# Second FFN's seven-product phase: the block sums move from GpSimd to VectorE

## The chip, the cores and the metric

The kernel runs on one core of a Trainium2 chip. A core has TensorE for matrix products, VectorE and ScalarE for elementwise work, GpSimd for the same at a slower rate, and SyncE, whose queue starts the transfers from memory. Each engine works through its own queue of instructions in order, and engines wait for each other with semaphores. The metric is the device time of one execution in microseconds (us), the median of several runs.

## The reference

One transformer layer over 512 latent and 256 context tokens of width 1024, in float32: a half-step SwiGLU FFN, a token mixer (latent attention with eight heads beside a chunked gating MLP), and a second half-step FFN. Each is modulated by vectors that a third projection makes from a condition. Only the latent stream is returned. The part that matters here is the last:

```python
def swiglu(h, w1, w3, w2):
    return (jax.nn.silu(h @ w1) * (h @ w3)) @ w2

def ffn_sublayer(h_in, shift, scale, gate, norm_w, w1, w3, w2):
    h = modulate(rms_norm(h_in, norm_w), shift, scale)
    return h_in + 0.5 * gate * swiglu(h, w1, w3, w2)
```

In the second FFN, h has 512 rows, and w1 and w3 are 1024 x 2816, so there are 22 column tiles of 128 (NF = 22).

## The kernel before

**Split operands.** TensorE multiplies in a reduced form of float32. To keep the accuracy, every operand is split in two: ScalarE casts it to that form (the high part, tiles `oph`, `hh`, `gh`), and VectorE subtracts the high part from the original (the low part, `opl`, `hl`, `gl`). One product is three matmuls, high x high, high x low and low x high (`mm3`). `Stream.operand` does the two steps of a split for a piece of 128x512 weights; five pairs of operand tiles go round (`OPS = 5`). So splits can run at most five operands ahead of the products that use them.

**Seven products in place of eight.** For column tile f, w1 and w3 together form a 2 x 2 arrangement of blocks of 512 x 128 against the token halves and the depth halves. The class `Winograd` computes the four results with seven products. It needs sums of the weight blocks. With q[0] to q[3] the four 128x512 pieces of one loaded block, the sums are s1 = q2 + q3, then q2 = q0 - q2 (called s3), q0 = s1 - q0 (s2), and q1 = q1 - q0 (s4); each overwrites its piece, once the piece itself was split. On the other side the sums of activations (T1 to T4) are made once. The order of a unit's products in `unit` is T1, B21, T2, T3, then B11 of the next unit, then T4 and B22. T1 multiplies s1, B21 q1, T2 the new q0, T3 the new q2, T4 q3, and B22 the new q1.

**Slots.** `Flow` keeps a queue of wants, functions that each issue one split. Before the matmuls of each product, `Flow.slot` issues, in this order: the first part of the work that evacuates the product before, the splits for which operand tiles have come free, and the rest of the evacuation. The phase is recorded with `nc.ordered = "all"`, so that every engine's queue has the order of this program. Evacuation works on banks of 128x256: VectorE adds banks to each other (`u2`, `u3`, `ev_lo`, `ev_hi`), ScalarE applies silu and the cast of the result `gh`, VectorE makes `gl`. T4 accumulates into the bank of T3; it may start once `ev_u3` has read that bank.

**Who makes the sums.** In `wants`, `first` loads the block (`prep`) and gives GpSimd s1, and behind the split of q0 it gives GpSimd s3 and s2. `third` gives GpSimd s4 behind the split of q1. The first block of the second FFN (f = 4) is an exception: `wino.prep(NPLAIN2, nc.vector)` runs earlier, and its sums s1, s3, s2 and s4 go to VectorE. Column tiles 0 to 3 use plain products. Units 4 to 21 use the seven-product form. After units 4, 8, 12, 16 and 18, `down_flow` runs a down projection whose weights pass through the same wants; each takes 8 slots. In the last unit (`f + 1 == NF`) the order of products is T2, T3, B21, T1, T4, B22, and some matmuls of the final down projection stand among them, where the scheduler put them.

**Transfers.** A block is 1 MB, loaded by SyncE's queue (L127). Two block buffers exist (`BLOCKS = 2`), so the load for unit f + 2 waits until the last piece of unit f's block was split.

The first FFN has a phase of the same class, with 384 columns and GpSimd's sums. It is not part of the change.

The lines that the prediction's steps touch:

```python
    def split(self, dst, src, eng=None):
        self.pin(self.nc.scalar.copy(dst[0], src))
        self.pin((eng or self.nc.vector).tensor_sub(dst[1], src, dst[0].bitcast(F32)))
...
            def ev_u3():
                v.tensor_add(u3, W, u2)
                v.tensor_add(u3, Z, u3)
                yield
```

Of the kernel before, what the change touches and what calls it, by code (L numbers as in the profile page):

```python
# [21 lines left out]
NF = FF // P  # L22
# [151 lines left out]
def layer_kernel(ctx: ExitStack, tc: tile.TileContext, xT, wfirst, wst, wada, wuq, wkpe, cols, wrope, vnw, rope, out):  # L174
    nc = Core(tc)
# [6 lines left out]
    st = Stream(nc, raws, opp, OPS, wst)  # L182
# [81 lines left out]
    u0, rw0 = st.raw_pool.tile([P, 2048], F32, tag="block", bufs=BLOCKS, name="block_first"), st.raw()  # L264
# [48 lines left out]
    def ada_row(r, d, kts=range(NK)):  # L313
        n = 2 * P if d in ROWS2 else P
        o = pa[0:2, :n]
        for kt in kts:
            pin(nc.tensor.matmul(o, sc[:, kt, :], r[:, kt * n : kt * n + n], start=kt == 0, stop=kt == NK - 1))
        return o
# [83 lines left out]
    class SsqAcc:  # L402
        def __init__(self, pool, n, eng):
            self.pool, self.n, self.eng = pool, n, eng
            self.acc = None
            self.squares = []
# [122 lines left out]
    for k in range(NK):  # L529
# [13 lines left out]
        if later:  # L543
            o = ada_row(units[k + 2][0], k + 2)
# [121 lines left out]
    U_UP2 = U_IN + 22  # L666
# [11 lines left out]
    class Winograd:  # L678


        def __init__(self, pool, n, u0, blocks, g_tile, sl_bufs, s1_bufs):
            self.sl_bufs, self.s1_bufs = sl_bufs, s1_bufs
            self.ready = (None,)
            self.pool, self.n, self.u0, self.blocks, self.g_tile = pool, n, u0, blocks, g_tile

# [12 lines left out]
        def wants(self, f):  # L698
            q, s1, eng = [], [], []

            def first():
                if self.ready[0] != f:
                    self.prep(f)
                q[:], s1[:], eng[:] = self.ready[1], [self.ready[2]], [self.ready[3]]
                a = st.operand(q[0])
                if not self.ready[4]:
                    eng[0].tensor_sub(q[2], q[0], q[2])
                eng[0].tensor_sub(q[0], s1[0], q[0])
                return a

            def third():
                a = st.operand(q[1])
                eng[0].tensor_sub(q[1], q[1], q[0])
                return a

            of = lambda i: lambda: st.operand(q[i])
            return first, lambda: st.operand(s1[0]), third, of(0), of(2), of(3), of(1)

        def plan(self, flow, f0, downs, late=False):
# [139 lines left out]
    blocks = {"B11": hb(0, 0), "B21": hb(4, 0), "B22": hb(4, 384), "T1": hb(0, 384)}  # L859
# [51 lines left out]
    wino = Winograd(gp, 384, U_UP1, blocks, g_tile, 1, 4)  # L911
# [29 lines left out]
    for f in range(NFIRST, NPLAIN1):  # L941
        last = f == NPLAIN1 - 1
# [4 lines left out]
        for w in range(2):  # L947
            pair = None
            for g in (1, 0) if last else (0, 1):
# [12 lines left out]
                for k in range(NK):  # L962
                    c = slice(k % 4 * P, k % 4 * P + P)
                    a = [t[:, c] for t in pair[k // 4]]
# [660 lines left out]
    f2 = f2ctx.enter_context(tc.tile_pool(name="ffn2", bufs=2))  # L1625
# [74 lines left out]
    evac(0, 1)  # L1700
    diffs(3)
    blocks = {"B11": B11, "B21": B21, "B22": B22, "T1": T1, "T2": T2, "T3": T3, "T4": T4}
    wino = Winograd(f2, 256, U_UP2, blocks, g2_tile, 2, 2)
    wino.prep(NPLAIN2, nc.vector)
    flow = Flow(OPS)
    wino.plan(flow, NPLAIN2, lambda f: [(CHUNKS2[ci], U_DN2 + starts2[ci]) for ci in ends2(f)])
# [141 lines left out]
```

## Time and profile before

| | |
|---|---|
| median of 3 runs | 1158.27 us (1157.82 to 1159.63) |
| profiled execution | 1157.46 us |
| its span, first to last instruction | 1155.7 us |
| granted TensorE clock | 1.00 |
| TensorE busy | 1137.7 us (98%) |
| VectorE busy | 904.5 us (78%) |
| ScalarE busy | 532.7 us (46%) |
| GpSimd busy | 321.6 us (28%) |

The span is what the profile covers; the time of the execution has 1.76 us more around it. A group of instructions is written as engine, operation, output tile <- input tiles, shape, count, then busy time and the mean of one in ns. In the timeline the first column is the start in us from the span's beginning, the second the duration, and the bracket holds the idle time of the engine ahead of the instruction and what ended it. PE is TensorE, DVE VectorE, ACT ScalarE, POOL GpSimd. Most lines carry L60, the line of a helper that records every instruction, so groups are told apart by their tiles. In the windows each engine has its busy time in the stretch with the number of its instructions.

### The profile page before, as it was taken

The numbers are of one execution on the slowest core, as the hardware profiler recorded it, in microseconds if no ns is written. First come the engines' busy times: TensorE is split into PE (matmuls) and PEld (weight loads), VectorE is DVE, ScalarE is ACT, GpSimd is POOL, SyncE is SP. The second block draws the span as 40 slices with busy tenths as digits, with TensorE's granted clock in tenths as the row PEclk, the third lists the DMA queues.
The fourth block names the chain that finished last, engine by engine and source line by source line (L and its number), as shares of the span: only waits on it lengthen the run. The fifth ranks groups of instructions, "written<-read, shape, count | busy, mean of one in ns | idle before, by whom it ended". The sixth has DMA issues, their size and how long they took to land. (4 is left out here: it accounts for less than half of the span.)

```text
span 1155.7 us, 18702 instructions
## 1 busy us (share of the span) xinstructions
PE 1137.7 (98%) x7070; PEld 1069.7 (93%) x7070; DVE 904.5 (78%) x1670; ACT 532.7 (46%) x1075; POOL 321.6 (28%) x277
## 2 busy tenths in 40 slices
PE   9999999999999999999999999999999999999998
PEld 5699999999999999999988788999999989898997
DVE  4778989888988878867746969869876959686884
ACT  4454431441344213444735549876553535353441
POOL 0001402320433013300017636670013425152330
PEclk9999999999999999999999999999999999999999
DMA  9440244344234665312242101002221322233312
GB/s 346 150 157 24 92 146 147 109 145 154 103 128 146 222 205 170 133 64 68 83 146 91 57 35 56 20 1 76 72 92 55 134 86 77 106 110 110 110 37 92
DMA packets 34650, 125.89 MB, mean 109 GB/s; under 512 B 3584, under 2 KB 10496, under 8 KB 29056
## 3 DMA queue, kind: packets, MB, share of 16 engines
q1 hardware_dynamic: 34416, 124.63, 31.4%
q8 instruction: 56, 0.92, 0.3%
q14 instruction: 34, 0.28, 0.1%
q10 hardware_dynamic: 144, 0.06, 0.0%
HBM read 122.58 MB, written 2.10 MB: 108 GB/s over the span
## 5 line engine op out<-in xcount | busy, mean ns | idle before, releaser
L60 POOL TENSOR_TENSOR block<-block 128x512 f32<-128x512 f32 x69 | 104.9, 1520 | 395.8 <-DVE opl L60 393.1
L60 DVE TENSOR_TENSOR opl<-block,oph 128x512 fp32r<-128x512 f32 x216 | 184.0, 858 | 32.1 <-ACT oph L60 30.0
L60 ACT CAST oph<-block 128x512 fp32r<-128x512 f32 x216 | 133.8, 621 | 144.4 <-PE mm L60 99.1
L60 PE MATMUL mm<-gh,oph 128*128 128x384 f32 (+1 forms) x440 | 155.2, 353 | 0.0
L60 PE MATMUL mm<-gl,oph 128*128 128x384 f32 (+1 forms) x440 | 154.9, 352 | 0.0
L60 PE MATMUL mm<-gh,opl 128*128 128x384 f32 (+1 forms) x440 | 154.9, 352 | 0.0
L60 DVE SCALAR_TENSOR_TENSOR x<-mm,g,x 128x256 f32<-128x256 f32 (+2 forms) x184 | 82.8, 489 | 48.5 <-PE mm L60 47.8
L60 ACT CAST oph<-raw 128x512 fp32r<-128x512 f32 x106 | 64.5, 619 | 93.4 <-PE mm L60 74.5
L60 POOL TENSOR_TENSOR block<-s,block 128x512 f32<-128x512 f32 x35 | 48.2, 1378 | 153.8 <-DVE opl L60 153.1
L60 PEld LDWEIGHTS mm<-gh,oph 128*128 128x128 f32 x440 | 82.6, 188 | 5.7
L60 PEld LDWEIGHTS mm<-gh,opl 128*128 128x128 f32 x440 | 82.6, 188 | 5.6
L60 PEld LDWEIGHTS mm<-gl,oph 128*128 128x128 f32 x440 | 82.6, 188 | 5.5
L60 DVE TENSOR_TENSOR opl<-raw,oph 128x512 fp32r<-128x512 f32 x106 | 71.0, 683 | 11.7 <-ACT oph L60 11.2
L60 PE MATMUL mm<-hl,oph 128*128 128x384 f32 x192 | 64.3, 335 | 0.9 <-DVE hl L60 0.9
L60 PE MATMUL mm<-hh,oph 128*128 128x384 f32 x192 | 64.5, 336 | 0.0
L60 PE MATMUL mm<-hh,opl 128*128 128x384 f32 x192 | 64.1, 334 | 0.0
L60 DVE SCALAR_TENSOR_TENSOR junk<-raw,cb 128x1024 bf16<-128x1024 f32 x48 | 63.2, 1331 | 0.0
L60 POOL TENSOR_TENSOR s<-block 128x512 f32<-128x512 f32 x34 | 51.1, 1504 | 19.8 <-DMA block<-wst 19.8
L60 PE MATMUL one<-hh,oph 128*128 128x384 f32 x144 | 48.1, 334 | 0.0
L60 PE MATMUL one<-hl,oph 128*128 128x384 f32 x144 | 48.1, 334 | 0.0
L60 PE MATMUL one<-hh,opl 128*128 128x384 f32 x144 | 48.1, 334 | 0.0
L60 DVE SCALAR_TENSOR_TENSOR raw<-raw,cb 128x1024 f32<-128x1024 f32 x32 | 41.0, 1287 | 7.6 <-DMA raw<-wada 7.4
(649 smaller groups left out, 3462.7 us busy)
## 6 DMA issues: line engine op xcount, KB each, us to landing
raw<-wst SPq DMA_DIRECT2D x77, 512.0 KB, 3.7
block<-wst SPq DMA_DIRECT2D x36, 1024.0 KB, 4.9
raw<-wada SPq DMA_DIRECT2D x56, 512.0 KB, 4.1
block<-wada SPq DMA_DIRECT2D x7, 1024.0 KB, 7.2
x<-xT SPq DMA_DIRECT2D x6, 512.0 KB, 7.0
raw<-wfirst SPq DMA_DIRECT2D x8, 256.0 KB, 6.2
out<-x SPq DMA_DIRECT2D x7, 256.0 KB, 2.5
block_first<-wada SPq DMA_DIRECT2D x2, 512.0 KB, 8.1
```

The source lines that it names most:

```text
L60: return lambda *a, **k: self.tc.keep_in_program_order(f(*a, **k))
```

## The change

The second FFN's object of class `Winograd` gets `on_vector = True`. All four block sums of its units are then VectorE's, in other places of the program. s1 follows the split of the block's first piece; s3 follows the split of s1, s2 that of q1, and s4 that of the new q0. Each thus stands one want ahead of the split that reads it. In the last unit s1, s3 and s2 follow the first split together, since the order of products differs there. Everything that ScalarE and SyncE issue keeps its order. 68 sums leave GpSimd's queue (four for each of 17 units) and join VectorE's; unit 4's sums stay on VectorE and move by a slot.

```diff
     class Winograd:
-        def __init__(self, pool, n, u0, blocks, g_tile, sl_bufs, s1_bufs):
-            self.sl_bufs, self.s1_bufs = sl_bufs, s1_bufs
+        def __init__(self, pool, n, u0, blocks, g_tile, sl_bufs, s1_bufs, on_vector=False):
+            self.sl_bufs, self.s1_bufs, self.on_vector = sl_bufs, s1_bufs, on_vector
             self.ready = (None,)
             self.pool, self.n, self.u0, self.blocks, self.g_tile = pool, n, u0, blocks, g_tile
...
                 return a
             of = lambda i: lambda: st.operand(q[i])
+            v = nc.vector
+            def sum_s1():
+                s1.append(self.tmp("s1", 512, self.s1_bufs))
+                v.tensor_add(s1[0], q[2], q[3])
+            def sub(d, a, b):
+                v.tensor_sub(q[d], s1[0] if a is None else q[a], q[b])
+            s3, s2, s4 = (2, 0, 2), (0, None, 0), (1, 1, 0)
+            last = f + 1 == NF
+            def first_v():
+                if self.ready[0] == f:
+                    q[:], s1[:] = self.ready[1], [self.ready[2]]
+                else:
+                    r = st.block(wst, (self.u0 + 2 * f) // 2)
+                    q[:] = [r[:, i * 512 : i * 512 + 512] for i in range(4)]
+                o = st.operand(q[0])
+                if not s1:
+                    sum_s1()
+                if last:
+                    sub(*s3)
+                    sub(*s2)
+                return o
+            def then(src, *d):
+                def want():
+                    o = st.operand(src())
+                    if d:
+                        sub(*d)
+                    return o
+                return want
+            if self.on_vector:
+                S1, Q = lambda: s1[0], [lambda i=i: q[i] for i in range(4)]
+                if last:
+                    return first_v, then(S1), then(Q[1], *s4), then(Q[0]), then(Q[2]), then(Q[3]), then(Q[1])
+                return first_v, then(S1, *s3), then(Q[1], *s2), then(Q[0], *s4), then(Q[2]), then(Q[3]), then(Q[1])
             return first, lambda: st.operand(s1[0]), third, of(0), of(2), of(3), of(1)
         def plan(self, flow, f0, downs, late=False):
...
     evac(0, 1)
     diffs(3)
     blocks = {"B11": B11, "B21": B21, "B22": B22, "T1": T1, "T2": T2, "T3": T3, "T4": T4}
-    wino = Winograd(f2, 256, U_UP2, blocks, g2_tile, 2, 2)
+    wino = Winograd(f2, 256, U_UP2, blocks, g2_tile, 2, 2, True)
     wino.prep(NPLAIN2, nc.vector)
     flow = Flow(OPS)
     wino.plan(flow, NPLAIN2, lambda f: [(CHUNKS2[ci], U_DN2 + starts2[ci]) for ci in ends2(f)])
```

## The prediction

> **What bounds the kernel now.** I read the page's busy shares first, then busy time by stage over the second FFN, then VectorE's timeline of one unit, then the instruction groups of the same stretch.
>
> ```profile
> PE 1137.7 (98%) x7070; PEld 1069.7 (93%) x7070; DVE 904.5 (78%) x1670; ACT 532.7 (46%) x1075; POOL 321.6 (28%) x277
> ```
>
> TensorE is busy for 98% of the span; the changed stretch has to be seen alone. A unit is one column tile f of the second FFN in the seven-product phase: seven products T1, B21, T2, T3, B11 (of the next unit), T4, B22. Units come in stretches of 4, 4, 4, 2 and 3 (f 5 to 21), with down projections between them; f 4 stands alone before.
>
> ```profile
> core 0: us, PE busy (x) PEld busy (x) DVE busy (x) ACT busy (x) POOL busy (x), PEclk, DMA share, GB/s
> 880.95:922.26 41.31, 40.93 (x338) 40.46 (x336) 35.93 (x61) 22.08 (x46) 18.68 (x13) 1.00 0.30 105
> 944.04:985.39 41.35, 40.98 (x337) 40.45 (x336) 35.99 (x61) 22.10 (x46) 18.60 (x13) 1.00 0.30 105
> 922.26:944.04 21.78, 21.78 (x98) 18.02 (x97) 12.23 (x20) 5.80 (x12) 4.16 (x3) 1.00 0.27 93
> 1070.32:1090.64 20.32, 20.32 (x169) 20.20 (x168) 17.04 (x29) 10.77 (x22) 6.83 (x5) 1.00 0.31 110
> 1101.55:1121.82 20.27, 20.27 (x169) 20.20 (x168) 16.88 (x29) 10.79 (x22) 7.85 (x6) 1.00 0.15 53
> ```
>
> Windows: the first two rows are stretches of four units, the third the down projection between them, the last two the two-unit stretch and the first two units of the three-unit one. The granted clock is 1.00 throughout. TensorE's own pace and its late places stand in its timeline:
>
> ```profile
> 896.78 0.28 PE L60 MATMUL one<-b11h,oph 128*128 128x256 f32 x1
> 898.32 0.36 PE L60 MATMUL mm<-t4h,oph 128*128 128x256 f32 x1
> ...
> 906.90 0.28 PE L60 MATMUL one<-t3h,opl 128*128 128x256 f32 x1
> 907.02 0.28 PE L60 MATMUL mm<-b11h,oph 128*128 128x256 f32 x1
> 908.34 0.28 PE L60 MATMUL mm<-b11h,opl 128*128 128x256 f32 x1
> 908.82 0.36 PE L60 MATMUL one<-t4h,oph 128*128 128x256 f32 x1 [0.20 <-DVE u L60]
> ...
> 917.53 0.28 PE L60 MATMUL one<-b11h,oph 128*128 128x256 f32 x1
> 919.31 0.35 PE L60 MATMUL mm<-t4h,oph 128*128 128x256 f32 x1 [0.18 <-DVE u L60]
> ```
>
> Matmuls start 0.12 us apart, so a product of 12 takes 1.44 us and a unit of seven 10.08. T4 is late: due at 908.34 + 0.12 = 908.46, it starts at 908.82, because its bank is still read by the addition `u`, which VectorE does late. From the first matmul of B11 to that of T4 the three late units of this stretch take 1.54, 1.80 and 1.78, which is 0.10, 0.36 and 0.34 too long. A stretch of four units should take 28 x 1.44 = 40.32 us and takes 41.31 to 41.35: 1.0 lost, the 0.80 just read and some 0.06 at each restart. Two units should take 20.16: 0.16 lost in 20.32, 0.11 in 20.27. In all 3 x 1.02 + 0.16 + 0.11 = 3.3 us. No gain from this change can be larger.
>
> One whole unit on VectorE, from the addition u = bank + p to the next such addition:
>
> ```profile
> start us, us, engine line op out<-in xcount [idle before <-releaser]
> 907.33 0.41 DVE L60 TENSOR_TENSOR u<-one,p 128x256 f32<-128x256 f32 x1
> 907.67 0.67 DVE L60 TENSOR_TENSOR opl<-s,oph 128x512 fp32r<-128x512 f32 x1
> 908.27 0.87 DVE L60 TENSOR_TENSOR u<-one,u 128x256 f32<-128x256 f32 x2
> 909.05 1.28 DVE L60 TENSOR_TENSOR opl<-block,oph 128x512 fp32r<-128x512 f32 x2
> 910.53 0.43 DVE L60 TENSOR_TENSOR one<-one,u 128x256 f32<-128x256 f32 x1 [0.20 <-PE one L60]
> 911.00 0.43 DVE L60 TENSOR_TENSOR one<-one,sl 128x256 f32<-128x256 f32 x1
> 911.34 0.70 DVE L60 TENSOR_TENSOR opl<-block,oph 128x512 fp32r<-128x512 f32 x1
> 911.96 0.41 DVE L60 TENSOR_TENSOR gl<-one,gh 128x256 fp32r<-128x256 f32 x1
> 912.30 0.41 DVE L60 TENSOR_TENSOR one<-one,u 128x256 f32<-128x256 f32 x1
> 913.05 1.16 DVE L60 TENSOR_TENSOR opl<-block,oph 128x512 fp32r<-128x512 f32 x1 [0.34 <-ACT oph L60]
> 914.13 0.42 DVE L60 TENSOR_TENSOR one<-one,u 128x256 f32<-128x256 f32 x1
> 914.99 0.43 DVE L60 TENSOR_TENSOR gl<-one,gh 128x256 fp32r<-128x256 f32 x1 [0.44 <-ACT gh L60]
> 915.51 2.38 DVE L60 TENSOR_TENSOR opl<-block,oph 128x512 fp32r<-128x512 f32 x2
> 917.82 0.41 DVE L60 TENSOR_TENSOR u<-mm,p 128x256 f32<-128x256 f32 x1
> ```
>
> This unit took 917.82 - 907.33 = 10.49 us, 0.41 above TensorE's 10.08. In the middle of a stretch VectorE's queue sets the pace; in the down projection it is busy 12.23 of 21.78 us and catches up, which is why the first unit of a stretch loses nothing.
>
> **The change, part by part.** GpSimd's four block sums of a unit go to VectorE. Their two prices:
>
> ```profile
> L60 DVE TENSOR_TENSOR opl<-block,oph 128x512 fp32r<-128x512 f32 x106 | 95.5, 909 | 14.6 <-ACT oph L60 12.7
> L60 DVE TENSOR_TENSOR opl<-raw,oph 128x512 fp32r<-128x512 f32 x36 | 24.3, 682 | 1.1 <-ACT oph L60 0.9
> L60 POOL TENSOR_TENSOR block<-block 128x512 f32<-128x512 f32 x33 | 50.4, 1527 | 145.5 <-DVE opl L60 144.2
> L60 ACT CAST oph<-block 128x512 fp32r<-128x512 f32 x106 | 65.7, 622 | 62.8 <-PE mm L60 43.2 <-PE one L60 16.1 <-DMA block<-wst 3.4
> ...
> 840.69 0.69 DVE L60 TENSOR_TENSOR opl<-block,oph 128x512 fp32r<-128x512 f32 x1
> 841.30 0.68 DVE L60 TENSOR_TENSOR block<-block 128x512 f32<-128x512 f32 x1
> 842.01 1.67 DVE L60 TENSOR_TENSOR block<-s,block 128x512 f32<-128x512 f32 x1
> ```
>
> Groups between 849 and 1150 us, then VectorE's timeline at 840 us, where the first block's sums already run on VectorE. *Removed:* GpSimd's instructions, and with them the slowing of VectorE's splits: 909 ns a split from the block, 682 where GpSimd is idle. *Added:* four 128x512 sums on VectorE, 0.68 us alone (841.30). Consecutive independent instructions overlap: two splits last 1.28, so the second starts 0.60 after the first, and that is what a sum takes of the queue; directly behind the sum that it reads it takes 0.71 (841.30 to 842.01). A 256-wide addition takes 0.34 (907.33 to 907.67).
>
> Steady unit, from 10.49 us: the splits at 913.05 and 915.51 ran beside GpSimd. They take 914.13 - 913.05 = 1.08 and 917.82 - 915.51 = 2.31, against 0.60 and 1.21 alone: -1.58. The idle 0.20 (VectorE waiting for TensorE) and 0.34 (for a split whose block came late) fill up once VectorE is the late one: -0.54. Four sums: 4 x 0.605 = +2.42. That is 10.79.
>
> To it comes a wait that is new. The sum q0 = s1 - q0 is written just ahead of the split of q0, and VectorE's queue holds nothing between the two. "One slot ahead" is a slot of the program; with VectorE behind, it is no time. ScalarE's cast must follow the sum, and the split's subtraction the cast. The row at 914.99 shows such a round trip: idle 0.44 for a 256-wide cast (0.37). For 512, with the 0.62 of the cast row, 0.69 idle, and the overlap of 0.08 is lost too: +0.77. Behind the waiting split stand the sum for q1 and the two additions that T4's bank and gate output need. The other sums have an addition or another split between them and their reader; I take their waits at nothing and the cover is VectorE's own work of 0.34 to 0.9 us; uncovered, each costs up to the same 0.77. Steady period: 11.56, so 1.48 us behind TensorE per unit.
>
> Who pays: T4 of the second, third and fourth unit of a stretch. The first of them pays less by what is left of the lead (up to five operands), 0.27 (before, the first lost 0.16 and the second 0.43, with 0.06 to 0.07 for the restart): 1.21. The middle: 1.48. The last has a plain down operand where a sum would stand ahead of `u`, so 0.60 less: 0.88. Sum 3.57, less 1.02 lost already: +2.55, three times +7.65. The two-unit stretch has one such T4, first and last at once: 1.21 - 0.60 = 0.61, less 0.16: +0.45. The last three units have one, in the second; there the last block's three sums are issued together, two dependent ones at 0.71 more: 0.61 + 1.42 = 2.03, less 0.11: +1.9. Unit 4, the last unit (matmuls of the final down projection stand among its own) and the down projections pay nothing: their cover is VectorE's 9 idle us per projection; gone, a unit would cost 1.48.
>
> Queues: SP's order is unchanged. Each block load still waits for VectorE's last split of the block two before. The chain that ended last shows how long it takes from there:
>
> ```profile
> 896.94 4.89 DMA block<-wst
> ```
>
> A unit that stretches to 11.56 us gives the load more time, so I cost it at nothing; if it came as late as the 0.34 seen at 913.05, it would cost 0.34 a unit. ScalarE's order is unchanged; GpSimd has nothing else to do here, so its relief itself brings nothing.
>
> Sum: 7.65 + 0.45 + 1.9 = **+10.0 us**. The profiled execution took 1157.46 us (span 1155.70 and 1.76 around it), the median of the runs 1158.27, 0.81 above: 1167.5 on the first, 1168.3 on the second.
>
> Bounds: without the new round trip each late T4 is 0.77 cheaper: stretches of four 0.44 + 0.71 + 0.11 = 1.26, +0.24 each; two units 0, so -0.16; three units +1.15: +1.7. With a second round trip exposed in each unit: (3.57 + 2.31 - 1.02) x 3 + 1.2 + 2.7 = +18.5. I take the middle value, because the program's order puts exactly one sum next to its reader.
>
> **A rule weighed.** The splits beside GpSimd grow by 909 - 682 = 227 ns on average, far less than a GpSimd sum's 1527. The Trainium skill, "SBUF — State Buffer", section "SBUF: two separate sides", says that VectorE with two SBUF inputs and a GpSimd instruction reading SBUF exclude each other for a whole instruction. Were VectorE blocked for each sum's whole 1.5 us, the relief of four would be 6 us against 2.42 added, and the time would be that of the first rival below. The trace bears out contention, but not of that size; the measured rows decide.
>
> **The rivals.** (1) *Faster:* GpSimd's brake on VectorE is larger than those two splits show. It decides if the relief per steady unit exceeds 2.42 + 0.77 - 0.54 = 2.65 us instead of 1.58. Then T4 is never late: 1158.27 - 3.3 = 1155.0. For it: the two splits at 915.51 took 1.10 us more than alone. Against: that is already counted, and 841.30 shows the sum's own price. 5%. (2) *The slot ahead holds* and no round trip shows: +1.7, 1160.0. For it: before, ScalarE waits idle for most casts, so it is ready. Against: ready or not, it cannot cast before the sum. 7%. (3) *Two round trips per unit*, when the sum of s1 or q1 also meets its reader: +18.5, 1176.8. For it: VectorE is late by more than a slot. Against: additions stand between. 8%. My forecast, between 1163 and 1173: 80%.
>
> **How the numbers follow.** Less than 0.2% (2.3 us) can't be told from no change here. Rival 1 is faster (0.05); rival 2 at +0.15% is no change (0.07, of which 0.01 may be slower); the rest, 0.89, slower. The range 1163 to 1173 leaves out the three rivals. Its width: the price of 512-wide instructions in the queue, known to 0.015 us, is 11 x 0.015 = 0.17 per unit, about 2 us in 11 late units, and half a round trip more or less is 3 to 4.
>
> **What would show it.** VectorE busy near 10 us of every 11.5 in the middle of a stretch, splits at 0.68 throughout, the period from u to u near 11.6, T4 late by some 1.2, 1.5 and 0.9, an idle time of 0.7 before one split per unit put down to ScalarE's cast, stretches of four at 43.9 us, down projections at 21.8 as before. Wrong would be: splits still at 0.9 without GpSimd, a T1 or T2 late for its own operand, or a late block load.

## The result and the profile after

The changed kernel takes 1169.82 us (median of five runs, 1168.13 to 1170.17), the kernel before in the same comparison 1159.18. The ratio is 1.0086 [1.0074, 1.0098]: slower by 10.6 us. The profiled execution took 1168.18 us with a span of 1166.1, against 1157.46 and 1155.7: 10.7 and 10.4 more. From the first matmul of unit 5 to the end it is 285.4 us against 274.7, so the changed phase alone accounts for 10.7. I use this stretch (span less the start of unit 5's first matmul) for single executions below, because the start of unit 5 itself moves by some 3 us from one profile to another (880.3 to 883.4).

The first line of the profile's page, after:

```profile
PE 1137.6 (98%) x7070; PEld 1069.4 (92%) x7070; DVE 920.3 (79%) x1738; ACT 530.8 (46%) x1075; POOL 223.1 (19%) x209
```

VectorE has 68 instructions more and GpSimd 68 fewer, as the change says. VectorE's busy time grows by 15.8 us only: the 68 sums at 0.68 would be 46, and the splits give much of it back. The windows of the changed kernel, two stretches of four units, the down projection between them and the two-unit stretch:

```profile
core 0: us, PE busy (x) PEld busy (x) DVE busy (x) ACT busy (x) POOL busy (x), PEclk, DMA share, GB/s
880.65:924.71 44.06, 40.98 (x337) 40.46 (x336) 38.05 (x74) 21.69 (x46) 0.00 (x0) 1.00 0.29 98
946.50:990.56 44.06, 40.98 (x338) 40.45 (x337) 38.05 (x74) 21.70 (x46) 0.00 (x0) 1.00 0.28 98
924.71:946.50 21.79, 21.79 (x99) 18.02 (x97) 13.54 (x23) 5.78 (x11) 0.00 (x0) 1.00 0.28 94
1078.20:1099.02 20.82, 20.37 (x170) 20.20 (x169) 17.70 (x34) 10.70 (x22) 0.00 (x0) 1.00 0.30 105
```

TensorE's work is the same (40.98 us of a stretch); each stretch of four is 2.7 longer and the whole of it is TensorE standing still. The down projection is where it was, 21.79. The places where TensorE stands, in its timeline:

```profile
896.48 0.28 PE L60 MATMUL one<-b11h,oph 128*128 128x256 f32 x1
899.14 0.36 PE L60 MATMUL mm<-t4h,oph 128*128 128x256 f32 x1 [1.05 <-DVE u L60]
...
907.84 0.28 PE L60 MATMUL mm<-b11h,oph 128*128 128x256 f32 x1
910.75 0.36 PE L60 MATMUL one<-t4h,oph 128*128 128x256 f32 x1 [1.32 <-DVE u L60]
...
1125.76 0.28 PE L60 MATMUL one<-b11h,oph 128*128 128x256 f32 x1
1129.26 0.36 PE L60 MATMUL mm<-t4h,oph 128*128 128x256 f32 x1 [1.91 <-ACT oph L60]
```

B11 to T4 should take 1.44 us. It takes 2.66 and 2.91 here and 2.31 in the fourth unit: late by 1.2, 1.5 and 0.9, in all three stretches of four. In the last three units it is 3.50, late by 2.06; the row puts that down to ScalarE's cast, but T4 starts 0.14 us after the first of VectorE's two additions `u` is done (1128.70 + 0.42 in VectorE's timeline), as it does at 910.75 behind the one that ends at 910.61:

```profile
1128.70 0.88 DVE L60 TENSOR_TENSOR u<-mm,u 128x256 f32<-128x256 f32 x2
```

So it is the same wait.

One unit on VectorE, from the addition `u` = bank + p to the next:

```profile
908.65 0.42 DVE L60 TENSOR_TENSOR u<-one,p 128x256 f32<-128x256 f32 x1
...
911.58 0.68 DVE L60 TENSOR_TENSOR block<-s,block 128x512 f32<-128x512 f32 x1
913.01 0.69 DVE L60 TENSOR_TENSOR opl<-block,oph 128x512 fp32r<-128x512 f32 x1 [0.74 <-ACT oph L60]
913.62 0.69 DVE L60 TENSOR_TENSOR block<-block 128x512 f32<-128x512 f32 x1
...
918.87 1.49 DVE L60 TENSOR_TENSOR opl<-block,oph 128x512 fp32r<-128x512 f32 x2
920.27 0.42 DVE L60 TENSOR_TENSOR u<-mm,p 128x256 f32<-128x256 f32 x1
```

The period is 920.27 - 908.65 = 11.62 us. The sum s2 (`block<-s,block`) is directly followed by the split that reads it, which starts only after 0.74 us idle, waiting for ScalarE's cast. The period holds one other idle time, 0.44 before `gl`, which stood there before the change too. Each split now takes the time that it has with GpSimd idle, in the groups of the second FFN's phase (mean 686 ns, 909 before):

```profile
L60 DVE TENSOR_TENSOR opl<-block,oph 128x512 fp32r<-128x512 f32 x106 | 72.6, 686 | 16.2 <-ACT oph L60 13.6
L60 DVE TENSOR_TENSOR block<-block 128x512 f32<-128x512 f32 x35 | 24.0, 685 | 0.1
```

### The profile page after: what moved, and what is told of

Same layout as the page of the kernel before. It is cut to its first block, busy times and chain, and to the rows that moved or that the text cites. A ratio compares the mean times of both kernels' runs of the same rounds, so it can differ in the third digit from the quotient of the medians.

```text
span 1166.1 us, 18689 instructions
## 1 busy us (share of the span) xinstructions
PE 1137.6 (98%) x7070; PEld 1069.4 (92%) x7070; DVE 920.3 (79%) x1738; ACT 530.8 (46%) x1075; POOL 223.1 (19%) x209
## 5 line engine op out<-in xcount | busy, mean ns | idle before, releaser
L60 DVE TENSOR_TENSOR opl<-block,oph 128x512 fp32r<-128x512 f32 x216 | 162.0, 753 | 33.4 <-ACT oph L60 30.5
L60 POOL TENSOR_TENSOR block<-block 128x512 f32<-128x512 f32 x35 | 52.9, 1510 | 251.3 <-DVE opl L60 250.0
L60 POOL TENSOR_TENSOR block<-s,block 128x512 f32<-128x512 f32 x18 | 24.3, 1350 | 124.3 <-DVE opl L60 124.2
L60 ACT CAST oph<-s 128x512 fp32r<-128x512 f32 x36 | 22.4, 623 | 39.4 <-PE mm L60 23.7
```

Source lines behind the costliest of these rows:

```text
L60: return lambda *a, **k: self.tc.keep_in_program_order(f(*a, **k))
```

## The experiments

The theory on trial is that of the prediction: in the middle of a stretch VectorE's queue sets the pace; the sums lengthen it, the sum beside its reader adds an exposed round trip through ScalarE, and T4's bank pays because its addition stands behind all this. The rivals: the round trip is not what costs, since VectorE would merely wait elsewhere; GpSimd's brake on VectorE has another size than read; or VectorE simply has too much work, in whatever order.

**The sums left out.** What the stretch costs without any sum shows the ceiling. (Unit 4's s1, made earlier, stays.)

```diff
             def sum_s1():
-                s1.append(self.tmp("s1", 512, self.s1_bufs))
-                v.tensor_add(s1[0], q[2], q[3])
+                s1.append(q[3])
             def sub(d, a, b):
-                v.tensor_sub(q[d], s1[0] if a is None else q[a], q[b])
+                return
```

> The changed kernel with all block sums of units 5 to 21 and of unit 4 left out on every engine (s1 is simply the fourth piece; the products use unsummed weights), so VectorE keeps the splits and the bank additions and GpSimd does nothing. Theory A, VectorE's queue sets the pace: without the sums a unit is 11.6 - 2.4 - 0.8 = 8.4 us of VectorE's queue, below TensorE's 10.08, so no T4 is late, the stretches of four last 40.3 us and the profiled execution is near 1154.2 (before, 1157.5, less the 3.3 lost there). Rival B, the loss comes from engines waiting for each other in the seven-product order itself, whatever the sums are: T4 stays late by 0.4 to 1 us and the time stays near or above 1157.

Measured in one execution: 1153.81 us; 271.4 from unit 5 on, 3.4 less than before and 14.0 less than the changed kernel. Its first stretch of four:

```profile
core 0: us, PE busy (x) PEld busy (x) DVE busy (x) ACT busy (x) POOL busy (x), PEclk, DMA share, GB/s
880.33:920.64 40.31, 40.31 (x337) 40.30 (x336) 30.76 (x61) 22.71 (x46) 0.00 (x0) 1.00 0.33 115
```

TensorE runs without a gap, 40.31 us for 28 products. The prediction's 3.3 us was the whole gain to be had, and the 14.0 us come with the sums on VectorE and the waits that they bring.

**s2 ahead of another split.** s2 is issued before the split of q1 in place of after it, so one split lies between the sum and its reader. No instruction more or less.

```diff
-            def then(src, *d):
+            def then(src, *d, ahead=False):
                 def want():
+                    if ahead:
+                        sub(*d)
                     o = st.operand(src())
-                    if d:
+                    if d and not ahead:
                         sub(*d)
...
-                return first_v, then(S1, *s3), then(Q[1], *s2), then(Q[0], *s4), then(Q[2]), then(Q[3]), then(Q[1])
+                return first_v, then(S1, *s3), then(Q[1], *s2, ahead=True), then(Q[0], *s4), then(Q[2]), then(Q[3]), then(Q[1])
```

> The changed kernel with one swap: the sum s2 is issued ahead of the split of q1 instead of behind it, so that one split stands between s2 and the split that reads it. The same instructions, one place moved. Theory A with a round trip of 0.77 us in each unit: the idle time of 0.74 before the split of q0 goes, each late T4 comes 0.7 to 0.8 us earlier (1.2, 1.5 and 0.9 become about 0.4, 0.7 and 0.1), and of the 10.4 us lost about 6 to 8 come back: profiled near 1161. Rival B, the order of engines waiting for each other is the whole loss: all 10 us come back, 1157.5. Rival C, the load alone counts and waits fill up elsewhere: nothing comes back, 1168.

Measured: 1162.97 us, ratio to the kernel before 1.0041 [1.0027, 1.0055]; 278.8 from unit 5 on. The same place of VectorE's timeline and the first stretch of this kernel's windows:

```profile
908.88 0.41 DVE L60 TENSOR_TENSOR u<-one,p 128x256 f32<-128x256 f32 x1
...
910.41 0.88 DVE L60 TENSOR_TENSOR u<-one,u 128x256 f32<-128x256 f32 x2
911.21 0.68 DVE L60 TENSOR_TENSOR block<-s,block 128x512 f32<-128x512 f32 x1
911.80 1.52 DVE L60 TENSOR_TENSOR opl<-block,oph 128x512 fp32r<-128x512 f32 x2
...
919.89 0.42 DVE L60 TENSOR_TENSOR u<-mm,p 128x256 f32<-128x256 f32 x1
```

```profile
core 0: us, PE busy (x) PEld busy (x) DVE busy (x) ACT busy (x) POOL busy (x), PEclk, DMA share, GB/s
882.08:924.34 42.26, 40.99 (x338) 40.47 (x336) 38.08 (x74) 22.32 (x46) 0.00 (x0) 1.00 0.30 102
```

The idle 0.74 is gone: the first split follows the sum at once, and the pair takes 0.24 more than the 1.28 of two undisturbed ones, since the second still waits a little for its cast. The period falls from 11.62 to 919.89 - 908.88 = 11.01. T4 is late by 0.61, 0.86 and 0.26 in a stretch of four, each some 0.2 more than expected, by 1.45 in the last units and not at all in the two-unit stretch. Of the 10.7 us, 6.6 come back by moving one instruction. So the round trip is the larger part of the loss. The remaining 4.1 us, 1.4 of them in the last three units, I put down to VectorE's longer queue.

**GpSimd beside the splits again.** The changed kernel, with four additions per unit on GpSimd whose results nothing uses, three behind the first split of a block and one behind that of q1.

```diff
+            def beside(o, n):
+                for _ in range(n if self.on_vector and self.ready[0] != f else 0):
+                    nc.gpsimd.tensor_add(self.tmp("beside", 512, 2), o[0].bitcast(F32), o[1].bitcast(F32))
...
+                beside(o, 3)
                 return o
```

> The changed kernel with four more GpSimd additions per unit (128x512, reading the two parts of a split and writing a scratch tile that nobody reads), issued where the kernel before gave GpSimd its sums: three behind the first split, one behind the split of q1. The output is untouched. It measures GpSimd's brake on VectorE alone. Theory A with the brake as read from the kernel before, 1.6 us per unit: 11 late units and a little of the first ones pay, +18 to +25 us, profiled 1186 to 1193. Theory A with exclusion (a VectorE instruction with two SBUF inputs that meets a GpSimd addition waits until that one ends): up to 1.3 us for each of four, +30 to +45 us, 1198 to 1213. Rival D, the brake is small because GpSimd mostly found VectorE on bank additions: under +8.

Measured in one execution: 1207.02 us. That is inside the range expected if the two engines exclude each other, but the total doesn't decide, since TensorE's clock fell too (last section). From unit 5 on the kernel takes 37.7 us more than the changed one. T4's lateness grows by 22.2 of them, which would fit the smaller brake as well, and the other 15.5 are nearly all matmuls at the lower clock. The rows decide. GpSimd's and VectorE's timelines at one meeting:

```profile
910.84 4.57 POOL L60 TENSOR_TENSOR beside<-oph,opl 128x512 f32<-128x512 f32 x3 [3.96 <-DVE opl L60]
```

```profile
902.13 0.41 DVE L60 TENSOR_TENSOR u<-mm,p 128x256 f32<-128x256 f32 x1
...
912.59 3.36 DVE L60 TENSOR_TENSOR opl<-block,oph 128x512 fp32r<-128x512 f32 x2
915.88 0.41 DVE L60 TENSOR_TENSOR u<-one,p 128x256 f32<-128x256 f32 x1
```

Two splits that take 1.21 alone take 3.29 (912.59 to 915.88) and end 0.54 after GpSimd's last addition (915.41). The period at this place is 915.88 - 902.13 = 13.75 us, 2.13 more than without GpSimd. The kernel before shows the same in GpSimd's timeline, read beside VectorE's rows of the prediction:

```profile
912.37 1.30 POOL L60 TENSOR_TENSOR s<-block 128x512 f32<-128x512 f32 x1 [0.88 <-DMA block<-wst]
913.74 1.62 POOL L60 TENSOR_TENSOR block<-block 128x512 f32<-128x512 f32 x1
915.45 1.30 POOL L60 TENSOR_TENSOR block<-s,block 128x512 f32<-128x512 f32 x1
```

The split that began at 913.05, inside the first sum, ended at 914.21, 0.54 after that sum's end (913.67). The two splits from 915.51 ended at 917.89, 1.14 after the third sum's end (916.75): the same 0.54 and the 0.60 of one more split. So a split that meets a sum ends a fixed time behind it, whenever it began, and 0.54 is 0.14 less than it lasts alone: nearly all of its work is done after the sum. It holds the other way too: GpSimd's second sum, begun inside the split, lasted 1.62 instead of 1.30. The operations on VectorE beside that sum that have one input from a bank, at 914.13 and 914.99, kept their 0.42 and 0.43.

**Splits held back.** The number of operands that may stand ready, five, is lowered to 5, 4, 4 and 3 in the four units of a stretch (4 at the end of the shorter ones) and goes back to five in the down projection. No instruction more or less; splits move back in VectorE's queue.

```diff
+            flow_size = self.sizes.get(f)
+            if flow_size:
+                self.flow.size = flow_size
...
         for ci in ends2(f):
+            flow.size = OPS
...
+    wino.sizes = {5: 5, 6: 4, 7: 4, 8: 3, 9: 5, 10: 4, 11: 4, 12: 3, 13: 5, 14: 4, 15: 4, 16: 3, 17: 5, 18: 4, 19: 5, 20: 4, 21: 4}
```

> The changed kernel with splits held back inside a stretch: at most five operands are kept ready in a stretch's first unit, four in its second and third, three in the fourth, and five again in the down projection. Not an instruction more or less; splits and sums move later in VectorE's queue, behind the bank additions that T4 waits for, and are caught up in the down projection, where VectorE has some 9 us idle. Theory A, what is late is the addition in VectorE's in-order queue, not the operands, so the order in which the work stands decides: a fourth unit's T4 late by 0 to 0.3, the others by 0.2 to 0.6, stretches of four at 41.5 to 42 instead of 43.9, about 7 us back: profiled 1161 to 1163. Rival E, VectorE simply has too much to do in these stretches: the same 1168, the lateness only moves to other products.

Measured: 1162.5 us, ratio 1.0033 [1.0023, 1.0042]; 278.5 from unit 5 on, 6.9 of the 10.7 back. Windows of a stretch and its down projection:

```profile
core 0: us, PE busy (x) PEld busy (x) DVE busy (x) ACT busy (x) POOL busy (x), PEclk, DMA share, GB/s
880.48:922.42 41.94, 41.21 (x338) 40.55 (x336) 36.74 (x72) 20.75 (x45) 0.00 (x0) 1.00 0.24 81
922.42:944.21 21.79, 21.79 (x99) 18.02 (x97) 14.64 (x25) 6.52 (x13) 0.00 (x0) 1.00 0.39 136
```

TensorE's timeline in the fourth unit:

```profile
916.72 0.38 PE L60 MATMUL mm<-t3h,opl 128*128 128x256 f32 x1 [0.22 <-DVE opl L60]
```

Two splits have gone from the stretch to the down projection (74 and 23 instructions become 72 and 25), which is no longer for them, 21.79. T4 of the second and third unit is late by 0.35 and 0.48. In the fourth unit it is now T3 that takes 0.57 too long: inside the product TensorE waits for the low part of the operand, held back too far, and not for a bank. That VectorE has too much work in all is therefore not the reason; it has too much ahead of the additions `u` in a stretch.

**The last unit's sums back to GpSimd**, in the changed kernel alone.

```diff
-            v = nc.vector
+            v = nc.gpsimd if f + 1 == NF else nc.vector
```

> The changed kernel with the last unit's four sums on GpSimd, all others on VectorE. It measures the one term of the last three units. Theory A: the T4 late by 2.06 us there (its block's three sums ahead of the addition) is late by 0 to 0.5 instead, and the span is 1.6 to 2 us shorter: 1164.3 instead of 1166.1. Rival: GpSimd's exclusion costs VectorE the same there, and nothing changes.

Measured in one execution: 1166.76 us, span 1164.9, 1.2 less than the changed kernel's. T4 in the timeline:

```profile
1125.64 0.28 PE L60 MATMUL one<-b11h,oph 128*128 128x256 f32 x1
1127.83 0.36 PE L60 MATMUL mm<-t4h,oph 128*128 128x256 f32 x1 [0.59 <-DVE u L60]
```

2.19 for 3.50, so T4 is 1.31 us earlier, near the 1.42 that the prediction put on the three sums of the last block. It is still 0.75 late where 0 to 0.5 was expected, and the span is 1.2 shorter, not 1.6 to 2. Part of the rival holds: in the changed kernel the three sums took 2.06 of VectorE's queue (1122.92 to 1124.98), and here two splits beside GpSimd's sums take 0.98 and 1.12 instead of 0.68, which is 0.74 more.

**All three together.** s2 moved, splits held back (5, 4, 4, 4), all four sums of the last unit on GpSimd.

> The swap of s2 and the split of q1, with four operands instead of five from the second unit of a stretch on, and the last unit's three sums that are issued together given to GpSimd. Theory A: what remains is T4 late by 0.3 and 0.7 in two units of a stretch of four; profiled about 1158.5, level with the kernel before. Rival E: near the 1163 of the swap alone.

Measured: 1159.7 us, ratio 1.0001 [0.9992, 1.0011], level with the kernel before, from which 0.7 us are still open from unit 5 on (275.5). T4 of the third and fourth unit of a stretch is late by 0.38 and 0.57.

The same, with the holding back set by the product in place of by the unit (four operands from T3 of a stretch's second unit on, its eleventh product, three from T4 of the third unit, its twentieth; the expectation counts from 0):

```diff
             flow = self.flow
+            flow.size = self.sizes.get(self.count, flow.size)
+            self.count += 1
             a = flow.take()
...
+    wino.sizes = {18: 4, 27: 3, 46: 4, 55: 3, 74: 4, 83: 3, 102: 4, 116: 4}
```

> As the run with the swap, the held-back splits and the last unit's sums on GpSimd, but each split held back at a chosen product: in a stretch of four, four operands ready from T2's neighbour in the second unit (product 10 of the stretch, B11 being the fifth of each unit) and three from product 19; in the short stretches four from product 10. Theory A: with the bank additions ahead and the operands still in time, T4 is late by under 0.3 us anywhere, the seven-product phase comes within 1.5 us of the run without sums, and the time is 1 to 2 us under the kernel before. Rival E: as the coarser version, level with the kernel before.

Measured: 1157.52 us (1155.83 to 1158.59), ratio 0.9988 [0.9979, 0.9997], a little faster than the kernel before, and 273.8 from unit 5 on, 0.9 less. Its first stretch of four:

```profile
core 0: us, PE busy (x) PEld busy (x) DVE busy (x) ACT busy (x) POOL busy (x), PEclk, DMA share, GB/s
881.06:922.05 40.99, 40.87 (x337) 40.45 (x336) 36.83 (x72) 20.76 (x45) 0.00 (x0) 1.00 0.25 83
```

This stretch is 0.3 us shorter than before, with all four sums on VectorE. It stays 0.7 above the stretch without sums, and 2.4 in all from unit 5 on, where at most 1.5 was expected: T4 of the third unit is late by 0.24, and T3 of the fourth takes 0.3 too long.

**The kernel before with splits held back**, 5, 5, 5, 4 and 5, 5, 4, 4 in a stretch.

> The kernel before, GpSimd's sums as they were, with one split held back in the fourth unit of each stretch of four (five operands ready in units one to three, four in the fourth). If order in VectorE's queue is what makes T4 late in the kernel before as well, the 0.4 us lost in each fourth unit goes: 1.2 us less, 1157.2 against 1158.4. If not, no change.

> As the run before, with four operands in units three and four. By theory A the 0.4 us lost in the third and perhaps the fourth unit become less: 1 to 2 us less than the kernel before, 1156.5 to 1157.5. A risk that it shows: a sum by GpSimd takes 1.3 us and needs its slot of lead, so the operands themselves may come late.

The first took 1156.43 us, ratio 0.9983 [0.9973, 0.9992], where 1.2 us were expected; the second 1159.34, ratio 0.9998 [0.9988, 1.0007], where 1 to 2 were. In the second, T4 of the third unit is in time but that of the fourth 0.78 late: the held splits come back there. In the first, T4 of the fourth unit is in time in all three stretches, as expected, and two of them are 0.3 us shorter than before (41.03 and 41.04). The first takes 41.55, because T4 of its third unit is 1.10 late: in the unit ahead two splits met GpSimd's sums and took 1.79 and 1.72. From unit 5 on the trace is only 0.2 us shorter than before's (274.5). So 2 us in the runs stand against 0.2 in the phase that was edited. The clock isn't the reason, since the runs at 1.00 alone differ as much (medians 1156.24 and 1158.22). I can't say where the rest comes from, and draw nothing from it.

One thing no run separates: the change gives the sums to another engine and to other places of the program at once. Only the last unit was tried with the new places and GpSimd.

## Why the prediction was right

The forecast was 1168.3 us in a range from 1163 to 1173; the runs gave 1169.82. Of the 1.5 us between them 0.9 is the kernel before itself, 1159.18 in this comparison and 1158.27 in the forecast's. By its steps:

- *The steady period*, 11.56: 11.62. The sums cost 0.60 of the queue each and the splits went back to 0.68, both as read from rows of before.
- *The round trip*, 0.69 idle and 0.08 of lost overlap: 0.74 idle. The program's order did tell which sum meets its reader: only s2 stands one want ahead of its split. s1 and s3 stand three ahead and s4 four, where the section on the change says one of each. What taking the wait away is worth was put too high: 0.61 a unit and not 0.77, because the pair of splits still loses 0.24. For 11 late T4 that is 1.8 us, and with the 0.55 of the restarts (below) it is why s2 moved leaves +4.1 from unit 5 on and not the lower bound's +1.7.
- *Who pays*: T4 late by 1.21, 1.48 and 0.88 predicted, 1.22, 1.47 and 0.87 measured; 0.61 in the two-unit stretch (2.05 - 1.44) and 2.03 in the last, 0.61 and 2.06 measured. That the middle one agrees to 0.01 is in part luck: the period was 0.06 longer than predicted, and 0.06 of what a unit loses falls not on T4 but on the restart behind it.
- *The sum*, +10.0: the stretches gained 2.73 each (7.65 predicted for three, 8.2 found), 0.50 for 0.45, 2.0 for 1.9. The 0.55 in the stretches is outside the three T4: 3.74 us lost in each, of which T4 accounts for 3.56, the rest 0.18 at restarts. The working left these restarts out of its 3.57 and yet took them off with the 1.02 lost already.
- *Nothing for the block loads and the down projections*: no split waited for a load, and the projections took 21.79.
- *The rivals.* The first (GpSimd's brake is worth more than the sums cost) fell: every split is back at its 0.68 and VectorE is still late. Its condition was also miscounted: a relief of 2.65 a unit only brings back the 10.49 of before, and T4 in time would need 3.06 (10.49 - 0.54 + 2.42 + 0.77 = 13.14, less TensorE's 10.08). The second (a slot is a lead) fell with the idle 0.74, and moving s2 showed what the lead would have been worth. The third (two round trips) fell: one new idle time per unit.

One reading was wrong. The part on the rule said that the trace bore out contention, "but not of that size". The Trainium skill, "SBUF — State Buffer", section "SBUF: two separate sides", says that VectorE with two SBUF inputs and a GpSimd instruction that reads SBUF keep each other out for the whole instruction. The rows at 913.05 and 915.51 and the run with GpSimd beside the splits agree with it, but for the 0.14 us of each split. The average of 227 ns said how seldom a split met a sum: much of GpSimd's time lay beside bank additions. The sum was not harmed, because its 1.58 of relief was taken from the two rows of the meeting and not from that rule multiplied by four sums.

## What to carry to other kernels

An instruction that changes engine is priced in the queue that receives it, in the stretch that sets the end, with who stands behind it; that TensorE was 98% busy and VectorE 78% said nothing of that. A lead counted in places of a program is no lead in time once the engine is late: put another instruction between a value and a reader that goes through a second engine, which here gave back 6.6 of 10.7 us. Before work is taken off an engine, look for slack in the stage next to it: holding prefetched splits back moved two of each stretch into a down projection and gave 6.9 us without a single instruction less, while in the kernel before the same step gave nothing clear. Where two engines exclude each other, count the meetings in the timeline; a mean over all instructions hides them.

## What the hardware showed beside this

In the run with GpSimd beside the splits TensorE's granted clock fell eight times, which no other trace here shows in this phase. The pause before the first fall, in TensorE's timeline:

```profile
900.52 0.28 PE L60 MATMUL one<-b11h,opl 128*128 128x256 f32 x1
904.22 0.36 PE L60 MATMUL mm<-t4h,oph 128*128 128x256 f32 x1 [3.42 <-DVE u L60]
```

Windows of 3.41 us, cut at moments when the clock changed, or whole windows away from them:

```profile
core 0: us, PE busy (x) PEld busy (x) DVE busy (x) ACT busy (x) POOL busy (x), PEclk, DMA share, GB/s
901.96:905.38 3.42, 1.16 (x10) 1.19 (x11) 3.38 (x8) 0.37 (x1) 0.00 (x0) 1.00 0.63 199
905.38:908.79 3.41, 3.41 (x19) 3.41 (x18) 2.62 (x6) 1.14 (x2) 1.31 (x1) 0.50 0.27 111
915.62:919.03 3.41, 1.45 (x13) 1.28 (x12) 3.38 (x8) 0.37 (x1) 0.00 (x0) 1.00 0.54 190
919.03:922.44 3.41, 3.41 (x19) 3.41 (x18) 2.61 (x5) 1.14 (x2) 1.60 (x1) 0.50 0.28 118
929.27:932.68 3.41, 2.04 (x18) 1.87 (x17) 3.33 (x7) 0.89 (x2) 0.00 (x0) 1.00 0.56 173
932.68:936.10 3.42, 3.42 (x22) 3.08 (x22) 3.06 (x7) 2.13 (x5) 0.00 (x0) 1.00 0.89 328
973.64:977.06 3.42, 0.86 (x8) 0.65 (x6) 3.42 (x5) 1.12 (x3) 1.73 (x2) 1.00 0.16 26
977.06:980.47 3.41, 2.54 (x12) 2.57 (x13) 2.61 (x6) 0.62 (x1) 1.49 (x1) 0.50 0.72 281
980.47:983.88 3.41, 3.41 (x18) 3.41 (x18) 3.35 (x7) 1.61 (x3) 0.11 (x1) 0.50 0.00 0
```

The clock fell to 0.50 at 905.38, 1.2 us after the restart, and matmuls then started 0.21 us apart and not 0.12, so that one pause costs more than its length. At 977.06 it fell before the restart (977.93) and stayed low for two windows. All sixteen changes of the clock between 905.38 and 1171.62 lie a whole number of 3.413 us apart. From unit 5 on, each of the eight such windows at 1.00 in which TensorE was busy for less than 1.5 us was followed by 0.50, and none with 2.04 us or more was. So the length of a pause alone doesn't tell. One of 2.24 us from start to start (915.74 to 917.97) lowered the clock here, one of 2.18 in the changed kernel (1127.08 to 1129.26) did not, and one of 1.85 did at 58.02 in the run with s2 moved and in no other trace.

The Trainium skill, "TensorE: Matmul & The Clock Gate", section "Part 1: The HAM clock gate", gives a free-running window of about 3.4 us and the fall to half after an idle one. The 3.413 us of this trace agree. But the window need not be idle: 1.45 us of matmuls between 915.62 and 919.03 did not keep the clock up.
